# Down-projection of a decoder block on one Trainium2 core: all 22 contraction tiles in seven products, every output tile summed, gated and stored once

## The chip, the cores and the metric

The kernel runs on one core of one Trainium2 chip, in one launch. The metric is the time of an execution on the device in microseconds (us). Three runs of the kernel before gave 660.95, 661.21 and 664.27 us; the median is 661.21.

The core's engines each work through a queue of their own in order: TensorE (PE; its weight loads are shown apart as PEld), VectorE (DVE), ScalarE (ACT), GpSimd (POOL) and SyncE (SP). Here SP issues the plain transfers (hardware queue q1), POOL the accumulating ones, which add what they bring to what lies at the destination (software queue q0). Matmuls write to PSUM, eight banks of 128 x 512 floats; all else lies in SBUF.

## The reference

One layer of a decoder block over 512 tokens of width 1024: modulated norm, an input projection for two kinds of attention heads, an output projection, a gated residual; then a gated MLP with a causal convolution of width 3. The change touches only the last matmul of it, the down-projection of the MLP:

```python
h2 = rmsnorm(x, norm2_w) * (1 + scale2) + shift2
up = causal_dwconv(h2 @ ffn_w_up, ffn_conv_w, ffn_conv_b)
a, b = jnp.split(up, 2, axis=-1)
x = x + gate2 * ((jax.nn.silu(a) * b) @ ffn_w_down)
```

`silu(a) * b` is 512 x 2816, `ffn_w_down` is 2816 x 1024. The contraction of 2816 is 22 tiles of 128.

## The kernel before

**Arithmetic.** All of it is float32. A matmul takes operands of a shorter format (`F32R`), so each operand is split into a high part and a rest, `split(src, hi, lo)`, and a product is made of three passes: high x high, high x rest, rest x high. The high part is a copy (on ScalarE or VectorE, chosen beforehand for each one), the rest a subtraction on VectorE. `split_acc` makes the rest in another way: the negated source is written to the place of the rest, and an accumulating transfer on POOL adds the source in the other form; this takes work off VectorE and puts one transfer of 256 KB on POOL's queue.

**Seven products.** The down-projection pairs contraction tile `k` with tile `k + PAIRS` and splits the tokens (0 to 255, 256 to 511) and the output columns (0 to 511, 512 to 1023) into halves. With `A` the activations and `B` the weights, each as a 2 x 2 block matrix, it forms the four output blocks with seven block products in place of eight (the Winograd form of Strassen's scheme). The code numbers them in the order P1, P2, P5, P6, P3, P7, P4. Each has, for a pair, an `A` operand of 128 x 256 and a `B` operand of 128 x 512, both split, and two chunks of 128 tokens (`c`), each of three matmuls with 512 columns. Each sum over the pairs stays in PSUM. P1, P6, P7 and P4 all go into the two banks `psA`, P5 and P3 into `psB`, P2 into `psC`. When a sum is needed by itself, `snap` copies it out (`y11` after P1, `y22` after P5, `y12` after P6) or subtracts it from an earlier copy (`y22` after P7).

Before, `PAIRS` is 10, so the seven products cover 20 of the 22 tiles. The last two tiles, f = 20 and 21, are done plainly (`down_in`, `down_mm`): each weight tile of 128 x 1024 is loaded whole into the pool `R`, split, and multiplied for eight output tiles (4 token tiles `t` x 2 column halves `j`), on top of the sums that stand in `psC`, `psB` and `psA`, and in a further pair of banks `psD`.

**Output.** `fold` adds the gated copies `y11`, `y12` and `y22` to the residual `x1`; at the end each of the eight output tiles is read from PSUM, multiplied by `gate2`, added to `x1` and stored. The last one, (3, 0), is done in two halves of 256 columns.

**Operands.** `b11`, `b21`, `tw` and `b22` are lists of 128 x 512 tiles, one per pair: the four blocks of `B` and, in `tw` and `b22`, the sums of blocks that the scheme needs, made in place by VectorE or by an accumulating transfer of the weights from DRAM. `sk` and `A21` hold the sums of blocks of `A`. Even pairs of P1, P2, P5 and P6 use `split_acc`. Tiles share 90 SBUF buffers of class `S`, 4 of class `R` and the 8 PSUM banks (class `P`).

**Order.** What sets the order of the work is not the program's loops. The class `_Plan` records every instruction, and `emit` issues them in an order that was planned elsewhere and lies in the file as packed text: `ORDER` (a permutation of all instructions) and `CHOICE` (for each, the first or the second engine). As each engine works in order, this list is the order of every queue:

```python
went = np.cumsum(unpack(ORDER, "<i2").astype(int)).tolist()
second = np.unpackbits(unpack(CHOICE, "u1")).tolist()
return [(self.ops[i], self.ops[i]["how"][second[i]]) for i in went]
```

A buffer is given out in that order too: an instruction that first writes a tile takes the buffer that has been free for longest, and waits for the last reader of what lay in it. The list of before has 6,944 places. Products overlap in it: matmuls of P3 stand between those of P6 and P7, and the plain matmuls of f = 20 and 21 are spread over the last 50 us.

All instructions come from one line of the kernel's text, L281, where `emit` calls the engine; views of the profile therefore tell instructions apart by engine, operation and shape, not by line.

Of the kernel before, what the change touches and what calls it, by code (L numbers as in the profile page):

```python
# [21 lines left out]
P = 128  # L22
# [3 lines left out]
NT = 4  # L26
# [36 lines left out]
c-oD72bdJa^LEwD-t7gBbYzYoASW3_kerktQKDi%5F{xeAQBAtBcli+DCs~Xi6Ek64iH6@=pi{MNK}w~z=hqJuK(LTd&{9d&-  # L63
Xq1?Ci{RcXf4jg}1tUV<_Ms<9uWfblwd{Qw#c9+LJ|JNoQhw)<{q~(M{PZ&*AAyi7;>f|2`GNcctj4FcrYv-
{$uVd5xw^Pr8k#s8F5H<vsMXO8#F|J5z2tB;`=Qv*A*IcSsSsC#6xk5$#9Q7+l|_?YLf&ob)K|6CcG<Je`v`DoQ=+P0`$)m3y)eckSsLjQIxc?t;b{DN
lcjBZcUyY!k1H>AaMomuaD7N)9~b#5YwIqD2qGQ+{fU>voxxjr);wO8iuu{FH%TCFkW4Pzgv;yzxUGHkHTkHI$u_7?kIwD-ua%z{3Uf<p&>$bW4={4xT
lY+~B7eBoq)mel1f!MPt<I;K)bEL8k+*x6#6nF^-
j5n9Ca&ha(q7_xKn^Pzt0`fNXH*qL;n$I6Z`Wn+`}7TrbFX(vAv~$T@k4($Npo30w<PH`$DtD@^Oash+P4X-
J!;5!x)|XVgU*C^PAfq=BpQC{4hqm|`eX{sgy7x#$;ZO_gXT?hit`Q5b0g>cwFOm<r+gCNyq8B%(+Agv_P-XtNPKT$Q@?qcp*|7-MBaF+cq-
H6bP2aL$;k@{qz^$wvVr{S5GVRtkddHPk(Ucd>Z8gkFR0W}?+qyr}~TmdAL{;hNw7XNKnG5@c}E==a}-  # L70
P6D`KawJ0z$ej@7qL`5zkat1Mj@Fb)czaQFU8XeAqp41RKt@Htiwhpg_}6FH^f1Nw4`f6`j#}UU0KM`?L!Jm}%3Cx-evW)Aa}nmUAZhzJhkC~%%VZY8l
Mj8C0Z%sc?@eh;--(6(i;&G171Qp>_L&(HO<n07sYAO!*{1Z!s+lR0BZ7jb%#0`_t9V)y*)Ed}Z95`17(v&_C-
I<~gf|vFLMP=ijg(KNDXhLdT0IxpAy7po(^Fxct^@t*#Y0d(IU*yY9qV@|)r+{^!FZW=MefKPB?o<jf=sO=I|VArl87<^rh%x@gocZ@u^PBv?Mn!Lir=
# [60 lines left out]
07@W;!Z*HIA;YBkNC9lv(VY9CpN7qd3OO<z__dBFvnDQO}ko0L$8IbK!V2(o2yh29%UIS9zrZfs-SZZnTYJuYhm^TZEX-
# [154 lines left out]
def hybrid_block(ctx: ExitStack, tc: tile.TileContext, x, par, ide, cst, adat0, adat, ada1, adag, wg0, wt, wn, ws,  # L289
# [1016 lines left out]
    def snap(pss, sub=None):  # L1306

        plan.sect, out_ = "dnf", sub or [u("sn") for _ in range(2)]
        for c in range(2):
            if sub:  # L1310
                V.tensor_sub(sub[c], sub[c], pss[c])
            else:
                copy(out_[c], pss[c])
        return out_

    def fold(op, ys, i, j):

        plan.sect = "dnf"
        for c in range(2):
# [193 lines left out]
```

## Time and profile before

| what | us |
|---|---|
| three runs | 660.95, 661.21, 664.27 |
| the profiled execution | 661.06 |
| its span, first to last instruction | 659.0 |
| TensorE matmuls busy | 651.9 |
| VectorE busy | 626.8 |
| ScalarE busy | 468.5 |
| POOL busy | 126.5 |

The profiled execution took 661.06 us, of which 659.0 is the span from the first to the last instruction; the 2.06 us around it are not seen in the trace. In the profile, a row of a view by stretches gives for each engine the busy time and, in brackets, the number of instructions that lie in the stretch. `P<-S,S` is an instruction that writes PSUM and reads two SBUF tiles; the name of a class stands for all its tiles. A note such as `[3.26 <-DMA S<-in_wd_dram]` says that the engine was idle for 3.26 us before that instruction, and what ended the wait. Matmuls are pipelined: their mean duration is longer than the distance from one to the next, so the pace is read from how many of them lie in a stretch.

### The profile page before, as it was taken

To read this page: it belongs to the slowest core of one execution; us is meant where nothing else is said; L and a number is where in the kernel's file an instruction comes from. 1 tells how busy PE (TensorE), PEld (TensorE's weight loads), DVE (VectorE), ACT (ScalarE), POOL (GpSimd) and SP (SyncE) were. 2 spreads that over 40 slices of the span, in tenths; PEclk is the share of its full clock that TensorE was granted. 3 is DMA by queue.
4 is the path that set the end of the run, shared out by engine and by line. 5 is a ranking of instruction groups with operands and counts; after the bars stand their busy time and mean duration, and the time that the engine had idled before them with its cause. 6 is when DMAs were issued, how large, how long until landed. Compare 5 with 4: busy or idle time off the path is not lost. (4 is left out here: it accounts for less than half of the span.)

```text
span 659.0 us, 12614 instructions
## 1 busy us (share of the span) xinstructions
PE 651.9 (99%) x4177; PEld 586.6 (89%) x4177; DVE 626.8 (95%) x1540; ACT 468.5 (71%) x1162; POOL 126.5 (19%) x148
## 2 busy tenths in 40 slices
PE   9999999999999999999999999999999999999996
PEld 9887888888988888988999999999999998888775
DVE  7999999988999999999999999999999999999897
ACT  6668896537679999646996466657768789987440
POOL 0001000011000014301113333333332432343200
PEclk9999999999999999999999999999999999999999
DMA  9998646575523579976648899989999999998603
GB/s 320 390 370 288 219 145 185 130 198 129 144 85 108 188 254 233 250 204 203 176 112 164 181 198 187 202 211 211 211 199 199 203 237 257 242 203 178 113 0 129
DMA packets 65609, 129.39 MB, mean 196 GB/s; under 512 B 11124, under 2 KB 11780, under 8 KB 65544
## 3 DMA queue, kind: packets, MB, share of 16 engines
q1 hardware_dynamic: 44920, 91.07, 41.3%
q0 software_dynamic: 20624, 37.52, 34.3%
q8 instruction: 33, 0.54, 0.3%
q14 instruction: 32, 0.26, 0.1%
HBM read 108.11 MB, written 3.41 MB: 169 GB/s over the span
## 5 line engine op out<-in xcount | busy, mean ns | idle before, releaser
L281 PE MATMUL P<-S,S 128*128 128x256 f32 (+5 forms) x3687 | 608.9, 324 | 0.7 <-DVE S L281 0.4
L281 PEld LDWEIGHTS P<-S,S 128*128 128x128 f32 (+3 forms) x3687 | 524.5, 190 | 54.8 <-DVE S L281 1.7
L281 DVE TENSOR_TENSOR S<-S,S 128x512 fp32r<-128x512 f32 (+12 forms) x477 | 240.4, 545 | 5.7 <-ACT S L281 2.2
L281 ACT ACTIVATE S<-S 128x512 fp32r<-128x512 f32 (+3 forms) x345 | 173.6, 548 | 53.2 <-DVE S L281 28.8
L281 ACT ACTIVATE S<-P 128x256 f32<-128x256 f32 (+4 forms) x197 | 79.2, 420 | 55.1 <-PE P L281 52.4
L281 ACT ACTIVATE S<-R 128x512 fp32r<-128x512 f32 (+2 forms) x161 | 90.4, 587 | 20.4 <-PE P L281 10.2
L281 POOL DMA_DIRECT2D S<-R x45 | 42.7, 1003 | 280.3 <-DVE S L281 131.6
L281 POOL DMA_DIRECT2D S<-in_wu_dram x63 | 57.1, 969 | 150.2 <-DVE S L281 79.6
L281 DVE SCALAR_TENSOR_TENSOR S<-S,C,S 128x511 f32<-128x511 f32 (+2 forms) x112 | 81.8, 744 | 0.8 <-ACT S L281 0.2
L281 DVE TENSOR_TENSOR S<-P,S 128x256 f32<-128x256 f32 (+3 forms) x126 | 67.3, 540 | 7.2 <-PE P L281 4.3
L281 DVE TENSOR_TENSOR S<-R,S 128x512 fp32r<-128x512 f32 (+2 forms) x107 | 62.3, 594 | 1.0 <-ACT S L281 0.5
L281 PE MATMUL P<-C,S 128*128 128x128 f32 (+3 forms) x285 | 50.8, 269 | 0.2 <-DMA S<-in_adat_dram 0.2
L281 ACT ACTIVATE S<-S,C 128x512 f32<-128x512 f32 (+1 forms) x70 | 44.0, 646 | 9.1 <-DVE S L281 7.8
L281 PEld LDWEIGHTS P<-C,S 128*128 128x128 f32 (+1 forms) x285 | 36.6, 145 | 7.7 <-issue 0.6
L281 DVE SCALAR_TENSOR_TENSOR S<-S,S 128x512 f32<-128x512 f32 x62 | 41.5, 685 | 0.6 <-PE P L281 0.5
L281 ACT ACTIVATE S<-P,C 128x128 f32<-128x128 f32 (+1 forms) x72 | 29.2, 443 | 15.2 <-PE P L281 11.9
L281 ACT ACTIVATE S<-S,s 128x128 f32<-128x128 f32 (+4 forms) x82 | 38.1, 496 | 2.1 <-DVE s L281 1.6
L281 DVE SCALAR_TENSOR_TENSOR S<-P,C,S 128x511 f32<-128x511 f32 (+3 forms) x52 | 32.9, 650 | 0.9 <-PE P L281 0.5
L281 POOL DMA_DIRECT2D S<-S x20 | 17.5, 935 | 46.7 <-ACT S L281 42.7
L281 ACT ACTIVATE S<-P,C,C 128x128 f32<-128x128 f32 (+2 forms) x38 | 18.2, 519 | 8.4 <-DVE C L281 3.2
L281 DVE TENSOR_TENSOR S<-S,P 128x256 f32<-128x256 f32 (+1 forms) x36 | 16.8, 467 | 2.3 <-PE P L281 1.7
L281 PE MATMUL P<-R,S 128*128 128x512 f32 (+2 forms) x72 | 18.7, 364 | 0.0
(79 smaller groups left out, 300.9 us busy)
## 6 DMA issues: line engine op xcount, KB each, us to landing
S<-in_adat_dram SPq DMA_DIRECT2D x64, 256.0 KB
S<-in_wu_dram POOLq DMA_DIRECT2D x63, 256.0 KB, 5.4
R<-in_wu_dram SPq DMA_DIRECT2D x23, 512.0 KB
S<-R POOLq DMA_DIRECT2D x45, 256.0 KB, 5.6
S<-in_wu_dram SPq DMA_DIRECT2D x42, 256.0 KB
S<-in_wd_dram SPq DMA_DIRECT2D x40, 256.0 KB
S<-in_adag_dram SPq DMA_DIRECT2D x32, 256.0 KB
R<-in_wn_dram SPq DMA_DIRECT2D x12, 512.0 KB
```

The costliest lines, as they stand in the source:

```text
L281: getattr(engines[eng], method)(*map(place, args), **{k: place(v) for k, v in kw.items()})
```

## The change

`PAIRS` goes from 10 to 11, so all 22 tiles go through the seven products. The plain part (`down_in`, `down_mm`, `psD`, the raw loads of f = 20 and 21) is removed. Each output block is finished by a new helper `finish` where its sum is complete in the program's text: `y11 + psC` for block (0, 0), `psB - y12` for (0, 1), `y22` for (1, 1), and `psA` for (1, 0). It multiplies by `gate2`, adds to `x1` and stores; `fold` is removed. In the last product, P4, the operands of the last four pairs (`TAIL`) are made first, then their matmuls run chunk by chunk, the second chunk in two halves of 256 columns, each finished and stored by itself.

`ORDER` and `CHOICE` are replaced. The new list has 6,966 places; its first 5,125 are those of the old one. Its last weight load (`b22[7]`) stands at place 6,572; in the old list the last one (`b22[9]`) stands at 6,700. The diff, without the packed texts and cut where nothing is changed in substance:

```diff
-    PAIRS, LATE = 10, 2
+    PAIRS, TAIL = 11, 4
...
-    def prod(pss, k, a, b_, first, acc=False):
+    def prod_in(a, b_, acc):
         plan.sect = "dnw"
-        w = plan.tile("S", (P, 512), F32R, "w"), u("wl", F32R) if acc else plan.tile("S", (P, 512), F32R, "w")
+        w = u("w", F32R), u("w", F32R)
         (split_acc if acc else split)(b_, *w)
         plan.sect = "down"
         x_ = u("da", F32R)
-        ah, al_ = x_[:, :256], x_[:, 256:]
-        split(a, ah, al_)
+        split(a, x_[:, :256], x_[:, 256:])
+        return x_, w
+
+    def prod_mm(ps, k, c, x_, w, first, n=slice(0, 512)):
+        ah, al_ = x_[:, c * P:c * P + P], x_[:, 256 + c * P:256 + c * P + P]
+        for i, (l_, r_) in enumerate(((ah, w[0]), (ah, w[1]), (al_, w[0]))):
+            T.matmul(ps[:, n], l_, r_[:, n], start=first and k == 0 and i == 0, stop=k == PAIRS - 1 and i == 2,
+                     skip_group_check=True)
+
+    def prod(pss, k, a, b_, first, acc=False):
+        ins = prod_in(a, b_, acc)
         for c in range(2):
-            for n, (l_, r_) in enumerate(((ah, w[0]), (ah, w[1]), (al_, w[0]))):
-                T.matmul(pss[c], l_[:, toks[c]], r_, start=first and k == 0 and n == 0, stop=k == PAIRS - 1 and n == 2,
-                         skip_group_check=True)
+            prod_mm(pss[c], k, c, *ins, first)
...
-    def fold(op, ys, i, j):
-
+    def finish(y, i, j, c, n=slice(0, 512)):
         plan.sect = "dnf"
-        for c in range(2):
-            x_ = x1[2 * i + c][j]
-            V.tensor_mul(ys[c], ys[c], gate2[j])
-            getattr(V, op)(x_, x_, ys[c])
+        t, x_ = 2 * i + c, x1[2 * i + c][j]
+        o = u("uy") if y.tensor.name.startswith("P") else y
+        V.tensor_mul(o[:, n], y[:, n], gate2[j][:, n])
+        V.tensor_add(x_[:, n], x_[:, n], o[:, n])
+        Q.dma_start(out[t * P:(t + 1) * P, j * 512 + n.start:j * 512 + n.stop], x_[:, n])
...
         prod(psC, k, A12[k], b21[k], True, k % 2 == 0)
+    for c in range(2):
+        plan.sect = "dnf"
+        V.tensor_add(y11[c], y11[c], psC[c])
+        finish(y11[c], 0, 0, c)
...
+    for c in range(2):
+        plan.sect = "dnf"
+        V.tensor_sub(y12[c], psB[c], y12[c])
+        finish(y12[c], 0, 1, c)
...
     snap(psA, y22)
-    for k in range(PAIRS):
+    for c in range(2):
+        finish(y22[c], 1, 1, c)
+    for k in range(PAIRS - TAIL):
         prod(psA, k, A22[k], tw[k], False)
-    for op, ys, i, j in (("tensor_add", y11, 0, 0), ("tensor_sub", y12, 0, 1), ("tensor_add", y22, 1, 1)):
-        fold(op, ys, i, j)
-    psD = [bank("psd") for _ in range(2)]
...
-    def down_in(f):
-        raw, w = load_raw(wd[f]), []
...
-    def down_mm(f, t, j, w, ah, al_, c=slice(0, 512)):
...
-            V.tensor_mul(tmp[:, c], psd[t, j][:, c], gate2[j][:, c])
-            V.tensor_add(tmp[:, c], tmp[:, c], x1[t][j][:, c])
-            Q.dma_start(out[t * P:(t + 1) * P, j * 512 + c.start:j * 512 + c.stop], tmp[:, c])
+    ins = [prod_in(A22[k], tw[k], False) for k in range(PAIRS - TAIL, PAIRS)]
+    for c in range(2):
+        for n in (slice(0, 256), slice(256, 512)) if c else (slice(0, 512),):
+            for k in range(TAIL):
+                prod_mm(psA[c], k + PAIRS - TAIL, c, *ins[k], False, n)
+            finish(psA[c], 1, 0, c, n)
```

More of the change, by code (lines that the diff above doesn't have):

```diff
@@ L69 @@
[L69 to L73, printed above, removed]
@@ new lines @@
+~drXLBT`7BPls&IKqXU>H5FjGk2W+e4g)n_SxB)=~P`^;jQZ4XiAM3?R*yK>%1R|q9(LfUL-
+|pq#ZFn>m?*@>9%Z_SMc<egxR<Mf1h&ccf}|{m~!Fnn*CiNy=kg+p}TmB^y_>nA7GrX<^R=dJIY3fq%`Wcvs9YzF3Cp^q&P}9qx~ovjqCfg6W5E9g`T2
+)5~R!&OJ^lB<)<z*SPXS%<bmwN-
+HY@M=6nlx_tD2GDMOdUkvw!=c8FKTbWTdpo3uz$Bom&p;F~Cm(4w=YDJRv#b*D_sK>d4kLL#UTMNl$+wVabD&`YZ1$D0W7BS2;Fdjn-
+BBpT(}>8gZN3D9sJV?}_DQglbO{0*8-FWEp(L2xKl%=`^cBPa^9P69<iI*NW;<9Zh@A~44>QXOk~3-fT~f|wDjP#DF78@VU|>RgQSn><ZLaUY-qQUTZV
+^1ZaAyd-i~ic%8BVLFCuUg{`Yv2uB7BPccNl`M5=tJFoCMf{S!Abn*z-
@@ new lines @@
+m}}#iR8roEi0)W~TQ%m=krhy(@zi>8!uRH3imvi5?h;vr?ax-=n4QbTO2y^HE)Ti}FZ-
+E5O%8(Oq4djE0_&tf)C#>hLGf`_1XSm$lbutEW3{9i}D0ZlJwB=c3OnPZf2CHR_N1bHP%&xs#v2=ZDVJuzjJmkiG)J_>kd4`GA)5&SV)7NOYpnZ+GcSN
+t7A(p&jqgwfP~u+)q5#c^5WbgQAeC>r6=>-
+FS<P_cgeap2d@7DBa{jdJF$S5o%DVz0nhD8djA$xUp`EM1m6;+aFcAD8hZz+eO(B)*>~U&Z=?huaGz61$>kyxJ&p^s|xxM7t_bkx1(a+TdIY=0sGht&)
+<R9tAT?QY;ml<&0A#{bk|^!{;H1Ck_~S}`lv5l1+P$)e$}6cRmb>!(e^a@Opu#=-
+^m;Z*Ei6rtUk}N`iwrI?oey@p033nML+2}EK*C}_EE)mdU>F+<I$FbYv5T+3tr9{`SXnanQQCGcsIbVrJ+Nm%i#-
+ZljXv<kct;*qi)XgtPHuZ{P_c!+^2XB=W>IA{dUFkqi#E1qm$sl&Z}t1N-
@@ new lines @@
+`^qyMJ>)D<bv0+}2m*d7iFIKr?Q0e(S?-
+x~JtuNLzE<7ots)D0Lv!vk<R5bocWaSgBp~TDmnm#U2vh6t*(7)Y=Av?aI?`)ab^wc{3e$4ohaNXAxa2uv9lTx&V}ONX&fymITBL&1?_%-
+3Q?12`*^u>mH-2sw!P|OR5c0RM%DqvCf5gm99dmZnR3W6rAA#I=gyI-
+{Hp~DVw<@#fOznttlqz$VV59{OTVh8&{H#xf`(#@kuJ}dg!klpVE1OPl}5m;@cy&184PlH@neVpjVP>IyY~{44=|Z(`;*L-
+ogA5EUh7lFmac<;9iwKSxXF?nB#FBkT~nfuzu(xi0}8P*G=z`2J{O(EgMvB-
+I@!)8%AiCZ^9DiP(k`Y8aXFbd0kDeswt4)5ju|Isg6@82>ce>9SA~yVx1~#JO{~qO48H%3w|-
+UA=Fa`XcE6mi>0fciqde%eo6Y+VvTXm;DGtf7EBCn(}l6Z&vPx?ey1(3hr6!$#z|9p(Mpq|@95Xi_`rJlTqXnUd<Bm8<7pV<J|7RYQ)}EDnAt~xEAp9B
@@ new lines @@
+5xum|;%g=3%L7ePP&#-pgQ1U>gh{?D;3y-
+tN(sx6u%dZw^v)!B9XK8rd&P2;w^q#QY*UU^etnW*d_aXPYq)vLz_aX))O^HkfZxety@<8(PSn2Bxq`X5L6vWWf;-FQ5;%BjL3W#Z1`U<qN`w-pD9-
+X_0C(9c6##rhrOX)V=zl?81eyHC-
+r1?0oaI9_fIrWK{o_takOD{6}F<yTU+{3C}dcXNOJ2ZWT)un>z)Gm}a4TjWr=rMVk*^l>Y_@%}QnBQvh6R+15xF#fhy39vZdXh?@WM{;p<jxUmQ)W50)
+K<O0u95lN)l(rWLzBa4OayqHY-aqM%@8(?cqaMhh!)9{v6k)a&hHJ|rmN)Tv0`*OLCXC@4iDIj;5#-
+G{1Q3Pp|{24b_d84uuI3(c^L|<aWH+JH{9$2vkUd7wRRI_j~+=?fh-
+%+D*49NdXi_#Jiq<|$Z$Qs<qrF<zP(=rwAVul@p)}5Xd&oSeScrU`)tq)(MxUl46Pt?|InYWrMo{Xlck84cc2~9*^9(mleaVY8h(vGYK=AY_G8&*1kC+
@@ new lines @@
+k@KO&Y#_AyZHb36(Jtt-ur?<U!gzq=!5nBD{&e{rzGkGALYIY)djGlrB+{Qg(tjX34y*)=e-
+Mch}N7;8%A#2&`pst9>v^Z>gLB614fL>qZ)nce0Z?h>kWB@!*J)3o7pIY{*GWhKZ{M>J1EFs&>`6S9Dec3hHJhOKU-
+P|XJ596o^o{Pu`UJS|1OZj1^cFIc@WqX>HBz0sp{DQZeS{RW@v+$$Ik!-
+BXT>4Ev%`0V#j^syP*x1>}=mpwA#qGN{aQzY<ZWZqTpi0sXdS&cOCojiG2J?=m1ihT1=!}?%Vq6A31|WTo&CPd}X^^Gb62(;|v$X@8L}RS1(DYSi|BbW
+A0GUFUv<^&mChA$BaRIfK-
+C@mBb5Soc=M?^X7j&mYp?xpwIi|aPl$XuRPmBEW6y4OG2w`dhzfcNMN+~WON&aa9v+w)~@UPjEFi&YdE)lkLDPp0gfeMYEHj=&EU8R`zat&S6YFh%Ln-
+&&9?Ex|}=RU#%A;-f|7t!m#Dg8*kq@&`!e?0xI+24-lw5Qc#^r`3n%(55#4B1YiS@3+`DlMhcavJwVA*W_{-
@@ new lines @@
+rFzgY;DtMT>C)EytcP=EPM8|5o~ZfnFWb9v%M!-
+sE#iwEz%Kyk<iD}EfTOLP4Vx$&>uS9T8AdGl^RM9T5mk79#4ybN2i<q5p^7pZdRsCS=%28AAUs}3|7qgg#EC*W_HVD6l|@rx7C2u*Yh@=rm@+ry?%@?1
+L<`_<X8@PWG@|&y8fvQgIBx2`Yez~^PNMp@wAc*KU$@);VgC3Eg{=!2o;i=*1Ma?y_R2^$x6i}scfIRa-5vkk9vH@ueHmrWfdUOC%C(ODV+>It@n7-
+?ngHiv##?Y-<7zLy$_-68#$*7bJ~u=vnE@c&d)3U-
+Ew?iNq;+u&dO5IQcu63=5g_KpZ~J1&h4RLW;gsCO}GAVmU#JQv)AL*s;rK<$$nplsDgh&Yc4E)1xh=qut+*1zNw!<rsBkK+MJk~C4K)>w|<c(YO7nup1
+t|^ry~4on)i5<%uZIU(@B|K$bvd;rg`nzn0|;Ddh$%Y4fcE<^eU_D=1n@EdXL049(%nkgr}@)DNV~t7-
@@ new lines @@
+IVadIP@5%lpLuJ!O|LPO!)+C(zn;eVb<T*E%aLWf!_UlY8s8q2DoNV&tc}5S0VoG-u+sA%gz}vDIxkrANW9-
+<S8TSGeP^U?!lf*}%Zd^f+E(CH16SLVTADjAwT29K1Uvcclg_cP(gfCaMHvHw#j>8d3b`b{@dW;Nve+9Z^&S{fe0c;3M|os;t*sD;sea1wNdl+q$EFO5
+dES4WlISb`KW8XS!$|pdOgt6?+P}s>P?u`sL-aoHj{AXwwq-
+FmM0HvFAVyf9C@22I!`KnI}V%X2=6E`QH9C2U-+kb@L<fX8R=9mz`MUs)&U;VWs;5F%Fg-pe_vknSB>mwt?^Ftokt6(2wL(dZ35H9u>yCE?W*6ibnu3G
+@#t{K(x$}TZpw!YjeKX1z)%0cQfS1WLw9I7gG$vJPa=R4EmZRk)Sz<-
+fvrJkFaOzy*&Ddz)v1`CQ3nACgUZ4r^Ucjm*puj92;u?KVzb%uJ*qzZNMjGv)_4b&M6Z;+LP%EIeL~lqFqbqr`dPeg%PJo9h-
@@ L184 @@
 c-muNfPnxOMg~%V11^aMBGtix08~`~36>B59156Xj0_?`n;IOT90-Py5J!73u;6tlir1K+E>vKGc>)F?mM>@k8O!0(F*%J<!T=`6%7o-
[L185 to L186 removed]
+QY~JHQ7hu9A!2pji7IXoqj~Wo73JeJh2VgP+U?;*uf&*r{0;+ie*j&d5brc6wPXp8fCPa)mpa%t7s!+fYzARXMiQ!`woGH=)H4GduLkeoW1Gbb(C?Y7x
+9sp><5Z(
 """
@@ L1366, in hybrid_block @@
     snap(psA, y22)
-    for k in range(PAIRS):
+    for c in range(2):
+        finish(y22[c], 1, 1, c)
+    for k in range(PAIRS - TAIL):
         prod(psA, k, A22[k], tw[k], False)
-    for op, ys, i, j in (("tensor_add", y11, 0, 0), ("tensor_sub", y12, 0, 1), ("tensor_add", y22, 1, 1)):
-        fold(op, ys, i, j)
-    psD = [bank("psd") for _ in range(2)]
-    psd = {(2 * i + c, j): ((psC, psB), (psA, psD))[i][j][c] for i in range(2) for j in range(2) for c in range(2)}
-    plan.sect = "down"
@@ L1375, in down_in @@
-    def down_in(f):
-        raw, w = load_raw(wd[f]), []
-        for j in range(2):
-            w.append((plan.tile("S", (P, 512), F32R, "w"), plan.tile("S", (P, 512), F32R, "w")))
-            split(raw[:, j * 512:j * 512 + 512], *w[j])
-        ah, al_ = u("ah", F32R), u("al", F32R)
-        split(act[f], ah, al_)
-        return w, ah, al_
-    def down_mm(f, t, j, w, ah, al_, c=slice(0, 512)):
-        (lh, ll), (rh, rl), o = (ah[:, toks[t]], al_[:, toks[t]]), (v[:, c] for v in w[j]), psd[t, j][:, c]
-        T.matmul(o, lh, rh, start=f == 2 * PAIRS and t > 1 and j == 1 and c.start == 0, stop=False, skip_group_check=True)
-        T.matmul(o, lh, rl, start=False, stop=False, skip_group_check=True)
-        T.matmul(o, ll, rh, start=False, stop=f == NF - 1, skip_group_check=True)
@@ L1390, in hybrid_block @@
-    for f in range(2 * PAIRS, NF - LATE):
-        ins = down_in(f)
-        for t in range(NT):
-            for j in range(2):
-                down_mm(f, t, j, *ins)
-    ins = [down_in(f) for f in range(NF - LATE, NF)]
-    for t, j in ((0, 0), (1, 0), (0, 1), (1, 1), (2, 1), (3, 1), (2, 0), (3, 0)):
-        last = (t, j) == (3, 0)
-        tmp = u("uy")
-        for a in (0, 256) if last else (0,):
-            c = slice(a, a + 256) if last else slice(0, 512)
-            for f in range(NF - LATE, NF):
-                down_mm(f, t, j, *ins[f - NF + LATE], c)
-            V.tensor_mul(tmp[:, c], psd[t, j][:, c], gate2[j][:, c])
-            V.tensor_add(tmp[:, c], tmp[:, c], x1[t][j][:, c])
-            Q.dma_start(out[t * P:(t + 1) * P, j * 512 + c.start:j * 512 + c.stop], tmp[:, c])
+    ins = [prod_in(A22[k], tw[k], False) for k in range(PAIRS - TAIL, PAIRS)]
```

197 lines of the change are left out of this document (81 added, 116 removed).

## The prediction

> **What bounds the kernel now.** I read the page's first part, then the table by stretches, then the timeline around the one place where TensorE pauses, the chain that ended last, and the timeline of the end.
>
> ```profile
> span 659.0 us, 12614 instructions
> PE 651.9 (99%) x4177; PEld 586.6 (89%) x4177; DVE 626.8 (95%) x1540; ACT 468.5 (71%) x1162; POOL 126.5 (19%) x148
> ```
>
> TensorE is busy for 99% of the span and VectorE for 95%. Both shares hide stages, so the next view cuts the part that the change touches. Its columns are the stretch, its length, then busy time and number of instructions of PE, PEld, DVE, ACT and POOL, the granted clock, the DMA engines' share and GB/s.
>
> ```profile
> 473.60:654.00 180.40, 179.95 (x1080) 160.30 (x1078) 176.77 (x357) 127.32 (x264) 51.58 (x59) 1.00 0.80 179
> 500.00:540.00 40.00, 40.00 (x336) 40.00 (x334) 39.45 (x79) 31.77 (x63) 14.85 (x17) 1.00 0.97 212
> 540.00:621.00 81.00, 81.00 (x383) 68.06 (x382) 79.47 (x172) 67.39 (x146) 28.01 (x32) 1.00 0.95 213
> 560.00:620.00 60.00, 60.00 (x266) 49.69 (x266) 59.54 (x129) 47.74 (x102) 22.62 (x26) 1.00 0.94 201
> 620.00:625.00 5.00, 4.61 (x20) 3.17 (x19) 3.43 (x8) 2.29 (x5) 0.00 (x0) 1.00 0.13 24
> 625.00:630.00 5.00, 5.00 (x24) 4.13 (x23) 5.00 (x10) 2.38 (x5) 0.00 (x0) 1.00 0.00 0
> 621.00:641.00 20.00, 19.61 (x83) 15.08 (x82) 19.43 (x39) 9.22 (x21) 0.00 (x0) 1.00 0.01 1
> ```
>
> The packed issue orders of the two kernels agree in their first 5,125 places, and behind them the old list has 1,078 matmuls. The row from 473.60 to 654.00 has that many (and two that overlap its edges), so the first 473.6 us stay as they are and all gains or losses fall behind that point.
>
> The row 560 to 620 is the down-projection at full pace: 266 matmuls of 512 columns in 60.00 us, 0.2256 us each. The row 500 to 540 is the up-projection: 336 of 256 columns in 40.00 us, 0.119 us each. A matmul costs by its columns, with 0.012 us more where 512 columns are cut in two (2 x 0.119 - 0.2256). The clock is 1.00 in every row. TensorE sets the pace; at that pace 20 us hold 88.7 matmuls, and the row 621 to 641 has 83. So 5.7 x 0.2256 = 1.28 us are lost to waits there. Most of it is one event: 620 to 625 has 20 matmuls, 625 to 630 has 24, and 4 x 0.2256 = 0.90 us. The timeline says why,
>
> ```profile
> 620.87 1.77 ACT L281 ACTIVATE S<-S 128x512 fp32r<-128x512 f32 x4 [3.26 <-DMA S<-in_wd_dram]
> 621.53 2.90 DVE L281 TENSOR_TENSOR S<-S,S 128x512 fp32r<-128x512 f32 x6 [1.93 <-ACT S L281]
> 623.22 30.73 PE L281 MATMUL P<-S,S 128*128 128x512 f32 x138 [0.39 <-DVE S L281]
> ```
>
> and the chain, in order of time:
>
> ```profile
> 612.64 8.15 DMA S<-in_wd_dram
> ...
> 620.87 0.64 ACT S L281
> 621.51 0.02 issue
> 621.53 1.64 DVE S L281 x3
> 623.17 0.04 issue
> 623.22 30.03 PE P L281 x132
> ```
>
> The last weight tile (`b22[9]`) is asked for at 612.64, when a buffer comes free, and lands 8.15 us later. ScalarE stood 3.26 us for it, VectorE 1.93 us, TensorE only the 0.90 us that its lead did not cover. After that the chain is TensorE to the end of the products.
>
> **Part 1, the matmuls.** Before: 10 pairs x 7 products x 2 chunks x 3 passes = 420, and 2 single tiles x 8 output tiles x 3 = 48, so 468 of 512 columns, six of them cut in two. After: 11 x 7 x 2 x 3 = 462, twelve of them cut in two. The number of instructions stays 474. Saved: 6 x 0.2256 = 1.35 us; six more cuts cost 6 x 0.012 = 0.07. Sum: **-1.28 us**, on the path, as TensorE has nothing else to wait for.
>
> **Part 2, the operand work on VectorE and ScalarE.** Counted from the two texts and the packed choices, the down-projection's VectorE work goes from 112 instructions of 512 columns and 120 of 256 to 102 and 128; ScalarE's from 99 and 64 to 105 and 74.
>
> ```profile
> L281 DVE TENSOR_TENSOR S<-S,S 128x512 fp32r<-128x512 f32 x53 | 35.3, 685 | 1.9 <-ACT S L281 1.9
> L281 DVE TENSOR_TENSOR S<-S,S 128x256 fp32r<-128x256 f32 x62 | 24.2, 417 | 0.1
> L281 ACT ACTIVATE S<-S 128x512 fp32r<-128x512 f32 x80 | 46.5, 621 | 13.9 <-DVE S L281 9.4 <-DMA S<-in_wd_dram 3.4 <-PE P L281 0.8
> L281 ACT ACTIVATE S<-S 128x256 fp32r<-128x256 f32 x56 | 20.9, 405 | 1.3 <-PE P L281 0.8 <-DVE S L281 0.4
> ```
>
> VectorE: -10 x 0.685 + 8 x 0.417 = -3.5 us. ScalarE: 6 x 0.621 + 10 x 0.405 = +7.8 us, into an engine that was idle for 13.6 of the 81 us from 540 to 621. Neither is on the path while its lead lasts, so I count both at nothing; without that cover the bounds are -3.5 and +7.8 us. VectorE, the nearer to its limit (79.47 of 81), gets lighter. The new early sums out of PSUM make no wait for it: in the new list `y11 + psC` stands 112 places behind the last matmul of product 2, and `psB - y12` 42 behind the last of product 3 in its chunk, and no operand of a matmul hangs on them. I take zero.
>
> **Part 3, the transfers.** Loads by SP bring the same bytes: 40 of 256 KB and two of 512 KB before, 44 of 256 KB after. The eleventh pair has an even number, so it adds four accumulating transfers on POOL for the low halves of products 1, 2, 5 and 6, and two that add a weight tile: 6 more than the 32 that POOL issues from 540 to 621.
>
> ```profile
> q0 software_dynamic: 4838, 8.80, 62.9%
> q1 hardware_dynamic: 4470, 8.40, 32.2%
> ...
> S<-S POOLq DMA_DIRECT2D x17, 256.0 KB, 5.8
> S<-in_wd_dram POOLq DMA_DIRECT2D x15, 256.0 KB, 7.9
> ```
>
> In that stretch POOL's queue took 62.9% of 81 us for 8.80 MB, that is 50.9 us for 33.6 transfers of 256 KB, 1.52 us each. Six more are **9.1 us of all sixteen engines**, in a stretch whose DMA share is already 0.95. From 621 to 641 the share is 0.01, so there is room behind. What of it reaches TensorE lies between nothing and 9.1 us. Nearest row: 81 us at share 0.95 cost TensorE 0.90 us, so I take nothing and keep the rest as a rival. By the Trainium skill ("DMA: Bandwidth & Descriptors", Specifications) the fabric moves 435 GB/s, which would make such a transfer 0.60 us and the six 3.6 us, an estimate; the trace's 1.52 us is two and a half times that, and I go by the trace.
>
> **Part 4, the wait at 621.** In the new order the last weight load stands 394 places from the end of the list; in the old one it stood 244 from it, in the middle of POOL's last transfers. No load is left that late, and the two whole 512 KB tiles with it are gone. I take the 0.90 us of that event as won, and leave the other 0.38 us of the 1.28: **-0.9 us**. Bounds: all 1.28 goes, or as much is lost elsewhere.
>
> **Part 5, the end.** From the timeline of the last microseconds:
>
> ```profile
> 650.76 3.19 PE L281 MATMUL P<-S,S 128*128 128x256 f32 x18
> ...
> 653.27 0.69 DVE L281 TENSOR_TENSOR S<-P,S 128x512 f32<-128x512 f32 x1 [0.19 <-PE P L281]
> 654.00 0.69 DVE L281 TENSOR_TENSOR S<-S,S 128x512 f32<-128x512 f32 x1
> 654.61 0.42 DVE L281 TENSOR_TENSOR S<-P,S 128x256 f32<-128x256 f32 x1
> 655.06 0.42 DVE L281 TENSOR_TENSOR S<-S,S 128x256 f32<-128x256 f32 x1
> ...
> 650.98 4.86 SPq L281 DMA_DIRECT2D out_dram<-S  x5
> ```
>
> TensorE ends at 650.76 + 3.19 = 653.95, VectorE at 655.48: 1.53 us, because only six half matmuls (0.7 us) stand behind the tile before the last one, whose gating takes 1.34 us (653.27 to 654.61). In the new code twelve half matmuls stand there (four pairs x three passes): 12 x 0.119 = 1.43 us cover the 1.34, and only 0.42 + 0.42 + 0.02 = 0.86 us follow TensorE. **-0.67 us**. The new order ends so: matmuls, then multiply, add and store of the last 256 columns. Behind it stay 659.0 - 655.48 = 3.5 us for the last 128 KB store. Five stores go out from 650.98 on, three of 256 KB and two of 128 KB; the last five of the new list are the same, so I leave it. All nine stores stand behind place 6,900 of the new list, which costs nothing: SP has no load behind them.
>
> **Sum.** -1.28 - 0.90 - 0.67 = -2.85. Span 659.0 - 2.85 = 656.15; the profiled execution took 661.06, 2.06 over its span, so **658.2 us**. The median of the three runs, 661.21, is 0.15 above that execution. A measurement of this kernel tells 0.5% (3.3 us) from no change, so faster means under 657.9 and slower over 664.5: my forecast lies just inside "no change".
>
> **Rivals.** (a) *All waits go.* VectorE is lighter by 3.5 us and the loads are earlier, so all 1.28 us vanish: 661.06 - 1.28 - 1.28 - 0.67 = 657.8, and down to 656.8 if the last store meets a quieter queue (1 of its 3.5 us, which is my allowance). For it: one cause made 0.90 of 1.28. Against: new orders bring small waits of their own. Chance 0.27.
>
> (b) *A new wait at the hand-over of a PSUM bank.* Products 6, 7 and 4 all go into the banks `psA`, and the result of product 7 must be read by VectorE before product 4 may go on. Before, 48 single-tile matmuls with banks of their own (48 x 0.2256 = 10.8 us of work) could be put into that gap; now only the shift between the two chunks covers it. Price, if nothing covers: a read of 0.675 us and one instruction of 0.68 us ahead of it, some 1.4 us for each chunk:
>
> ```profile
> 634.32 0.68 DVE L281 TENSOR_TENSOR S<-P,S 128x512 f32<-128x512 f32 x1
> 634.92 0.67 DVE L281 TENSOR_TENSOR S<-S,P 128x512 f32<-128x512 f32 x1
> ```
>
> That gives 658.2 + 1.4 to 2.8 = 659.6 to 661.0. Against it: six product matmuls of the other chunk hide 1.35 us each time. Chance 0.20. The Trainium skill ("Perfetto Trace Analysis", Matmul Optimizations) asks that all eight PSUM banks be used; the old code uses eight here, the new one six, so by that rule it would go this way. No run here shows it yet.
>
> (c) *Slower: the transfers become the pace.* Place: products 1, 2, 5 and 6, from 540 to 600, where the share is 0.95 and a transfer of 1.52 us takes 5.8 to 7.9 us to land, so a queue stands ahead of each. The four added transfers there delay all loads behind them by 4 x 1.52 = 6.1 us; it decides once that is more than the lead of the loads. Then 661.06 + 6.1 - 1.28 - 0.67 = 665.2. Against it: TensorE runs without a gap through the whole stretch, and ScalarE stood for a weight load 3.4 us in all. Chance 0.10.
>
> (d) *It doesn't save matmul time*, because the number of instructions stays at 474: if each cost the same whatever its columns, part 1 would be nothing and the time 659.5. The 0.119 us of the 256-column rows speak against it. Chance 0.03.
>
> **Numbers.** Forecast 658.2, chance 0.40 for 657.9 to 659.2. The range leaves out (c) and the far edges: 656.8 to 662.5. Faster by over 0.5%: (a) and a little of the forecast, 0.30. Slower: (c), 0.10. Within: the rest, 0.60.
>
> **What would show it.** Matmuls of the last stage 450 of 512 columns and 24 of 256; after 473.6 us no 5 us stretch with 20 matmuls where 24 fit; ScalarE's wait for `in_wd_dram` near 621 gone; VectorE ending 0.9 us behind TensorE. Wrong if TensorE shows gaps in 540 to 600 behind ScalarE or a transfer (c), or one behind a VectorE read of PSUM some 20 us before the end (b).

## The result and the profile after

The changed kernel takes 658.53 us (median of 20 executions), the kernel before 662.45 us on the same chip (20 executions): ratio 0.9943, 95% interval 0.9924 to 0.9962. That is 0.57% faster, or between 0.38 and 0.76%, where the forecast of 658.2 us stood for 0.46%. The bound of 0.5% lies inside the interval, so the runs don't say on which side of it the change falls. Nine of the 20 executions before and six of the 20 after are some 2.5 to 5 us longer than the rest, the six with a mean granted clock of 0.991 to 0.994 where the rest have 0.998 or more (no clock is on record for the 20 before); the medians of the rest are 661.31 and 658.29 us, which makes the change 3.0 us or 0.46%. The profiled execution of the changed kernel took 657.67 us, 1.77 of it around its span.

The page of the changed kernel begins so (busy time, share of the span and instructions of each engine), and its rows of the two busy DMA queues (packets, MB, share of sixteen engines) follow:

```profile
span 655.9 us, 12653 instructions
PE 648.8 (99%) x4177; PEld 584.7 (89%) x4177; DVE 623.1 (95%) x1537; ACT 474.0 (72%) x1179; POOL 132.0 (20%) x154
...
q1 hardware_dynamic: 45208, 91.07, 41.1%
q0 software_dynamic: 21488, 39.09, 36.3%
```

TensorE and VectorE are both down, by 3.1 and 3.7 us, with the same number of matmuls. ScalarE is up by 5.5 us and POOL has its six more transfers. The table by stretches (same columns as for the kernel before):

```profile
500.00:540.00 40.00, 40.00 (x333) 39.81 (x332) 38.47 (x77) 31.34 (x65) 15.18 (x18) 1.00 0.99 210
540.00:621.00 81.00, 81.00 (x384) 68.08 (x383) 80.91 (x179) 72.23 (x159) 28.82 (x33) 1.00 0.96 214
560.00:620.00 60.00, 60.00 (x266) 49.70 (x265) 59.92 (x136) 52.38 (x116) 23.63 (x27) 1.00 0.94 192
620.00:625.00 5.00, 5.00 (x23) 4.13 (x22) 5.00 (x13) 4.80 (x13) 3.21 (x4) 1.00 0.54 89
625.00:630.00 5.00, 5.00 (x23) 4.13 (x22) 5.00 (x10) 3.39 (x8) 0.33 (x1) 1.00 0.96 157
621.00:641.00 20.00, 20.00 (x90) 16.57 (x89) 20.00 (x40) 9.64 (x22) 3.54 (x4) 1.00 0.33 55
```

The row 620 to 625 had 20 matmuls and has 23; the row 621 to 641 had 83 and has 90, as many as fit. TensorE's busy time is the whole stretch in each row. In the column of VectorE one reads what became important later: 80.91 of 81 us. Before, it was 79.47, but 1.40 of the 1.53 us that were missing are VectorE's own wait for the late load (the 1.93 us that ended at 621.53). So VectorE was as good as full in this stretch in both kernels.

The timeline has one unbroken block of matmuls from 599.63 on, and the list of waits from 540 us (idle for, us in total, times, longest) has only 0.3 us in which ScalarE stands for a weight load, where 3.4 us stood before:

```profile
599.63 51.82 PE L289 MATMUL P<-S,S 128*128 128x512 f32 x239
```

```profile
ACT S L289 <- DMA S<-in_wd_dram: 0.3, 1, 0.3
```

The end, by the timeline:

```profile
647.77 3.67 PE L289 MATMUL P<-S,S 128*128 128x256 f32 x22
647.88 4.85 SPq L289 DMA_DIRECT2D out_dram<-S  x7
...
650.05 0.69 DVE L289 TENSOR_TENSOR S<-P,S 128x512 f32<-128x512 f32 x1 [0.33 <-PE P L289]
650.78 0.69 DVE L289 TENSOR_TENSOR S<-S,S 128x512 f32<-128x512 f32 x1
651.48 0.42 DVE L289 TENSOR_TENSOR S<-P,S 128x256 f32<-128x256 f32 x1
651.94 0.43 DVE L289 TENSOR_TENSOR S<-S,S 128x256 f32<-128x256 f32 x1
```

TensorE ends at 647.77 + 3.67 = 651.44. The gating of the tile before the last one (650.05 to 651.47) is done as TensorE ends, and VectorE ends at 652.37, 0.93 us behind. The chain that ended last says the same: TensorE alone from 249 us, then four instructions of VectorE.

```profile
249.24 400.80 PE P L289 x2764
650.05 0.70 DVE S L289
650.78 0.69 DVE S L289
651.48 0.44 DVE S L289
651.94 0.43 DVE S L289
```

**Where the time went.** Traces are compared from place 5,100 of the issue order, just ahead of where the two lists part, because the part before it, alike in all of them, took 471 to 476 us (the last section says why). In the table, "TensorE" is the time from the start of that instruction to the end of the last matmul, "lost" the sum of its pauses: the time by which a matmul started later than the steady pace of one behind another (0.2268 us with 512 columns, 0.1199 with 256), where that is over 0.03 us, and "tail" how long VectorE ends behind TensorE. They are worked out from the trace's records of single instructions.

| kernel | median, us | ratio to before on the same chip, 95% interval | TensorE, us | lost, us | tail, us |
|---|---|---|---|---|---|
| before | 662.45; 661.40; 661.66; 661.53 | | 182.46 | 1.25 | 1.54 |
| changed | 658.53 | 0.9943, 0.9924 to 0.9962 | 180.10 | 0.29 | 0.92 |
| e1_matmuls12 | 661.18 | 0.9992, 0.9963 to 1.0021 | 182.53 | 0.00 | 0.92 |
| e2_early_load | 659.73 | 0.9957, 0.9930 to 0.9984 | 181.07 | 0.00 | 1.54 |
| e3_acc6 | 660.52 | 0.9978, 0.9952 to 1.0004 | 184.93 | 4.98 | 0.93 |
| e4_dve6 | 661.74 | 1.0000, 0.9974 to 1.0027 | 183.86 | 3.78 | 0.92 |
| e5_tail6 | 659.22 | 0.9957, 0.9925 to 0.9989 | 181.56 | 1.63 | 1.53 |
| e6_handover | 659.79 | 0.9964, 0.9941 to 0.9986 | 182.08 | 2.20 | 0.93 |
| e7_dve6_late | 662.84 | 1.0006, 0.9977 to 1.0035 | 182.94 | 2.92 | 1.31 |
| e8_early_dve6 | 662.79 | 1.0021, 0.9994 to 1.0047 | 184.25 | 2.98 | 1.54 |
| e9_act6 | 658.92 | 0.9960, 0.9934 to 0.9986 | 181.36 | 1.40 | 0.93 |
| e10_dve3 | 659.39 | 0.9962, 0.9940 to 0.9984 | 181.60 | 1.32 | 0.92 |

The four medians of the kernel before belong to the changed kernel's runs, to e1 to e4, to e5 to e8, and to e9 and e10. They differ by up to 1 us, so a difference below between the medians of an experiment and of the changed kernel is good to 1 us at best, and the columns on the right carry the sizes. They come from one execution of each kernel.

From before to changed the span went down by 3.1 us: TensorE by 2.36, the tail by 0.62, and 0.13 lie ahead of place 5,100, where the lists are alike. The last store took 3.5 us in both. Of TensorE's 2.36, the cheaper set of matmuls is 1.28 (twelve of 512 columns fewer, twelve of 256 more: 12 x (0.2268 - 0.1199)) and the pauses are 0.96: the 1.25 us from 621 to 636 are gone, and three pauses of 0.1 us at 508 to 510 stand in this execution. The 0.12 that is left are delays under 0.03 us each. That is the whole difference; what the experiments had to tell was which edit stands behind each of these parts, and why the costs that the prediction counted at nothing stayed out.

### The profile page after: what moved, and what is told of

It reads as the page before. It is cut to its first block, busy times and chain, and to the rows that moved or that the text cites. A ratio compares the mean times of both kernels' runs of the same rounds, so it can differ in the third digit from the quotient of the medians.

```text
span 655.9 us, 12653 instructions
## 1 busy us (share of the span) xinstructions
PE 648.8 (99%) x4177; PEld 584.7 (89%) x4177; DVE 623.1 (95%) x1537; ACT 474.0 (72%) x1179; POOL 132.0 (20%) x154
## 4 chain that ended last, share of the span: by engine, by line
PE 93%; ACT 3%; DVE 2%; DMA 1%; SPq 1%; issue 0%
PE P L289 93%; ACT S L289 2%; DVE S L289 2%; DMA S<-in_adat_dram 1%; SPq L289 1%; ACT L289 0%; DVE s L289 0%; ACT s L289 0%; DVE C L289 0%
## 5 line engine op out<-in xcount | busy, mean ns | idle before, releaser
L289 DVE TENSOR_TENSOR S<-S,S 128x256 fp32r<-128x256 f32 (+12 forms) x484 | 241.0, 542 | 4.9 <-ACT S L289 1.5
L289 ACT ACTIVATE S<-S 128x512 fp32r<-128x512 f32 (+3 forms) x363 | 180.7, 546 | 57.1 <-DVE S L289 36.1
L289 ACT ACTIVATE S<-R 128x512 fp32r<-128x512 f32 (+2 forms) x156 | 87.6, 586 | 18.8 <-PE P L289 7.4
L289 DVE TENSOR_TENSOR S<-P,S 128x256 f32<-128x256 f32 (+3 forms) x122 | 64.8, 537 | 7.8 <-PE P L289 5.0
L289 DVE TENSOR_TENSOR S<-R,S 128x512 fp32r<-128x512 f32 (+2 forms) x103 | 59.6, 591 | 1.0 <-ACT S L289 0.5
L289 POOL DMA_DIRECT2D S<-S x24 | 21.5, 936 | 46.0 <-ACT S L289 28.1
L289 POOL DMA_DIRECT2D S<-in_wd_dram x17 | 17.4, 1207 | 18.2 <-DVE S L289 10.9
L289 DVE TENSOR_TENSOR S<-S,P 128x256 f32<-128x256 f32 (+1 forms) x38 | 18.2, 478 | 2.7 <-PE P L289 2.4
```

The lines of the kernel that those rows point to most:

```text
L289: getattr(engines[eng], method)(*map(place, args), **{k: place(v) for k, v in kw.items()})
```

## The experiments

All experiments run beside the kernel before; e2 and e8 are made from it, the others from the changed kernel. Where instructions are added, their results aren't read.

**e1_matmuls12: are TensorE's columns on the path?** Twelve matmuls of 512 columns behind place 6,600, into a bank that nothing else uses.

```diff
+    spare = bank("spare")
+    for _ in range(12):
+        T.matmul(spare, held[0][:, :P], held[1][0], start=True, stop=True)
     plan.emit(pools)
```

> The changed kernel with twelve matmuls of 512 columns more, into a PSUM bank that nobody reads, behind product 3's fourth pair (about 40 us before the end); nothing else is added. If the end is set by TensorE's columns (the theory behind the -1.28 us of the forecast): +12 x 0.2256 = +2.7 us on the span of 655.9, so 658.6, and no gap on TensorE. If other engines or transfers set the end and TensorE has slack beside them: less than +1 us.

TensorE takes 182.53 us in place of 180.10, 2.43 more, with nothing lost and the tail unchanged. The twelve follow one another at 0.226 to 0.227 us, 2.72 in all; the 0.29 that the changed kernel's profile lost at 508 to 510 us does not occur here, which is the difference. Its timeline has one block to the end:

```profile
559.78 94.20 PE L256 MATMUL P<-S,S 128*128 128x512 f32 x426
```

What is added to TensorE reaches the end in full. The saving of six matmuls' worth of columns is real, and that the number of instructions stays the same (rival (d)) doesn't matter.

**e2_early_load: was the late load alone the cause of the wait?** The kernel before, with its last weight load put into a buffer of class `R` and moved from place 6,700 to 6,489.

```diff
-        dst[k] = u("wd")
+        dst[k] = plan.tile("R", (P, 512)) if (k, j, f) == (9, 1, 19) else u("wd")
```

> The kernel before, with one edit: the last weight tile b22[9] gets a buffer of the class R, which has room there, and its load stands in the list behind that of b22[5], so it is asked for near 594 us and not at 612.6. VectorE, POOL and the matmuls stay as they are. If the wait at 621 came from that late load: no stretch near 621 with 20 matmuls where 24 fit, span 659.0 - 0.9 to 1.2 = 657.8 to 658.1. Rival, the wait was VectorE's fullness or POOL's bunched transfers from 608 to 613, and went because VectorE became lighter: the gap stays, span 658.7 to 659.2.

Nothing is lost on TensorE any more: 181.07 us, 1.39 less than before, and by the medians 1.7 us less. The rows of its table by stretches, 600 to 620 and 620 to 640, and the timeline:

```profile
600.00:620.00 20.00, 20.00 (x90) 16.58 (x89) 20.00 (x43) 14.04 (x31) 6.19 (x7) 1.00 0.84 144
620.00:640.00 20.00, 20.00 (x90) 16.54 (x89) 19.57 (x40) 7.06 (x16) 0.00 (x0) 1.00 0.00 0
```

```profile
599.65 52.38 PE L255 MATMUL P<-S,S 128*128 128x512 f32 x236
```

There are 90 matmuls from 620 to 640 where the kernel before has 84. VectorE has as much work as before and the tail is 1.54, so the wait goes by the load alone, with nothing taken off VectorE. The small losses at 632 and 635 us, which the prediction left standing, went with it: they were the same late load, seen further on.

**e3_acc6: how near are the transfers to being the pace?** The changed kernel with six more accumulating transfers of 256 KB on POOL (and three memsets of their destinations), at the places of products 1, 2 and 5: the change's own six doubled.

```diff
+    more = [plan.tile("R", (P, 1024)) for _ in range(3)]
+    for m in more:
+        G.memset(m, 0.0)
+    for i in range(6):
+        G.dma_start(more[i // 2][:, i % 2 * 512:i % 2 * 512 + 512], wd[i][:, :512], accum_op=OP.add)
     plan.emit(pools)
```

> The changed kernel with six accumulating transfers of 256 KB more on POOL's queue between products 1 and 6 (weights from DRAM, into spare buffers of class R that nobody reads), and three memsets on POOL ahead of them: as much transfer work again as the change added, 6 x 1.52 = 9.1 us of all engines. If the loads have a lead there (the forecast): span 655.9 to 656.9. If the transfers are near the pace (rival c): up to 4 x 1.52 = 6.1 us more, 658 to 662, with TensorE waiting between 560 and 610.

Median 660.52, 2.0 us above the changed kernel (2.3 by the two ratios). In the timeline VectorE stands 2.43 us for a transfer from `in_wd_dram`, and TensorE 1.80 us for VectorE:

```profile
570.47 1.70 DVE L256 TENSOR_TENSOR S<-S,S 128x512 f32<-128x512 f32 x4 [2.43 <-DMA S<-in_wd_dram]
...
574.10 4.45 PE L256 MATMUL P<-S,S 128*128 128x512 f32 x11 [1.80 <-DVE S L256]
```

```profile
574.00:578.00 4.00, 3.90 (x10) 2.75 (x11) 3.37 (x9) 3.42 (x7) 1.76 (x2) 0.57 1.12 247
578.00:582.00 4.00, 4.00 (x19) 3.29 (x18) 3.84 (x10) 3.19 (x9) 1.76 (x2) 1.00 1.09 223
```

In the rows by stretches behind that wait there are 10 matmuls in 4 us, then 19, and the granted clock is 0.57, then 1.00. So this profiled execution lost 4.98 us, more than the median. The way of rival (c) exists, and it opens with six transfers more than the change has; its price here is 2 us and not 6.1, since two loads in that stretch were late (issued at 562.81 and 564.39, waited for until 570.47 by VectorE and 574.58 by ScalarE) and not all. The run doesn't tell the DMA engines' share from POOL's own time: the six transfers and three memsets also took 11.1 us of POOL.

**e4_dve6 and e10_dve3: has VectorE room?** The changed kernel with six (e4) or three (e10) additions of 512 columns on VectorE, spread over the stretch from about 553 to 584 us.

```diff
+    for _ in range(6):
+        V.tensor_add(plan.tile("R", (P, 512)), x1[3][0], x1[3][1])
     plan.emit(pools)
```

> The changed kernel with six VectorE additions of 512 columns more (3.6 to 4.1 us, results that nobody reads), spread over places 6,100 to 6,350 of the list, that is over some 25 us of products 1 and 5: it gives VectorE back the 3.5 us that the change took from it. If VectorE has a lead over TensorE (the forecast counts the 3.5 us at nothing): span 655.9 to 656.4, and no gap. If its lightening is what removed the waits: TensorE waits again for VectorE, +1 to +4 us, 657 to 660.

> The changed kernel with three more additions of 512 columns on VectorE (3 x 0.69 = 2.1 us) at every other place of e4_dve6; their results are not read. If VectorE has no lead beyond some 0.5 us, about 1.6 us are lost (0.69 x 3 less the lead), 660.1 us, with pauses of TensorE that VectorE ends. If it has a lead of some 2 us that six additions used up, nothing is lost: 658.5.

e4 takes 661.74, 3.2 us more than the changed kernel, and TensorE 3.76 us more; e10 takes 659.39, 0.9 more, and TensorE 1.50 more. The additions are 4.2 and 2.1 us of work on VectorE. The rows from 560 to 600 of the changed kernel, then of e4, then the row from 560 to 580 of e10:

```profile
560.00:580.00 20.00, 20.00 (x90) 16.57 (x89) 20.00 (x44) 17.65 (x40) 7.74 (x9) 1.00 1.00 234
580.00:600.00 20.00, 20.00 (x90) 16.57 (x89) 20.00 (x49) 16.67 (x37) 8.90 (x11) 1.00 0.99 192
```

```profile
560.00:580.00 20.00, 19.15 (x82) 14.90 (x81) 20.00 (x41) 16.75 (x35) 7.43 (x9) 1.00 1.01 243
580.00:600.00 20.00, 19.51 (x85) 15.48 (x85) 20.00 (x49) 15.54 (x34) 8.44 (x10) 1.00 0.86 167
```

```profile
560.00:580.00 20.00, 19.81 (x86) 15.52 (x85) 20.00 (x42) 16.15 (x36) 6.45 (x8) 1.00 0.94 216
```

VectorE is busy for all of 20 us in each row, and TensorE goes from 90 matmuls to 86 and 82. The lists of waits name the engine (first e4, then e10; the changed kernel has no such row):

```profile
PEld P L256 <- DVE S L256: 4.8, 9, 0.9
```

```profile
PEld P L256 <- DVE S L256: 2.3, 6, 0.6
```

The expectation that a lead covers this falls. Worked out from single records, the shortest time between the end of an operand's split and the matmul that reads it was 0.4 to 0.7 us in each 10 us of the changed kernel from 550 to 620. That is VectorE's whole lead at the tightest operands, and 2.1 us of work more than use it up.

**e9_act6: is that so of any engine, or of VectorE?** The same places, but six copies of 512 columns on ScalarE (3.7 us).

```diff
+    for _ in range(6):
+        S.activation(plan.tile("R", (P, 512)), x1[3][0], AF.Copy)
     plan.emit(pools)
```

> The changed kernel with six more copies of 512 columns on ScalarE (6 x 0.62 = 3.7 us), spread over the same places as the six extra VectorE additions of e4_dve6; their results are not read. If only VectorE is level with TensorE, ScalarE (72% of the span) takes them: 658.5 us as without them, no new pause on TensorE, up to 0.5 us for copies that now come later. If any engine's work ahead of the matmuls counts in this stretch, because the operands are made just in time whoever makes them, the loss is as in e4_dve6: some 3 us, 661.5.

Median 658.92, 0.4 above the changed kernel. Of the 1.40 us lost in its trace 0.65 lie at 473 and 524 us, ahead of the copies; 0.53 at 565 fall among them, and 0.22 at 609 and 614 behind them. The row from 560 to 580, and the row of its list of waits that names ScalarE:

```profile
560.00:580.00 20.00, 19.74 (x88) 16.01 (x87) 20.00 (x42) 19.17 (x42) 6.99 (x8) 1.00 1.01 223
```

```profile
PEld P L256 <- ACT S L256: 0.7, 1, 0.7
```

ScalarE takes 3.7 us more for 0.4 us by the medians and 0.5 to 0.8 by the trace; VectorE took 4.2 us more at the same places for 3.2 and 3.8. The copies write the same buffers as the additions and read one of their two sources, so these are not the cause. ScalarE's share of part 2 was rightly counted at nothing.

**e8_early_dve6: was VectorE level before the change as well?** The kernel e2 (before, with the early load) with six additions on VectorE at the times of e4.

> e2 (the kernel before with the early load) with the same six VectorE additions at the same times as in e4, near 553 to 581 us. If the eleventh pair ate VectorE's lead there (5 us of splits and sums more in products 1, 2 and 5): e2 has more room than the changed kernel, 0 to +1 us. If VectorE stood level with TensorE before the change too: +3 to +4 us on e2, as in e4.

Median 662.79, 3.1 us above e2, and TensorE 3.18 us more. Its rows show the same picture as e4's:

```profile
560.00:580.00 20.00, 18.60 (x81) 14.69 (x80) 19.97 (x42) 16.99 (x36) 6.05 (x7) 1.00 1.03 257
580.00:600.00 20.00, 19.62 (x85) 15.54 (x84) 19.97 (x43) 16.05 (x33) 6.62 (x8) 1.00 0.82 170
```

So VectorE had no room in the old order either. Whether a change that took columns off TensorE and left VectorE's work as it was would have met that limit was not run.

**e7_dve6_late: is it so towards the end too?** The changed kernel with the same six additions at places 6,785 to 6,869, from 627 to 640 us.

> The changed kernel with the six VectorE additions of e4 placed late, between 627 and 640 us, where the change took the gating and folding away, so VectorE has the total of before again. e4 cost 3.2 us by the medians. If VectorE is a second limit that stands level with TensorE up to the end: +2.0 to +3.5 us here too. If e4 only hit a thin place in products 1, 2 and 5 and the end has room: 0 to +0.6 us.

The median is 662.84, but the executions spread from 659.88 to 666.28, so the trace is the better measure: from place 5,100 TensorE takes 2.84 us more and the tail 0.39, together 3.2. The timeline has TensorE standing for VectorE:

```profile
636.40 5.44 PE L256 MATMUL P<-S,S 128*128 128x512 f32 x20 [0.17 <-DVE S L256]
642.82 5.53 PE L256 MATMUL P<-S,S 128*128 128x512 f32 x23 [0.98 <-DVE S L256]
```

VectorE has no room here either: in neither of the two stretches tried, 553 to 584 and 627 to 640 us, is added work on it caught up.

**e5_tail6: does the number of half matmuls behind the second last tile set the tail?** Six of the last twelve half matmuls (places 6,946 to 6,951 of the unpacked list) are moved ahead of that tile's last ones, so that six stay behind it, as in the kernel before.

```diff
-order[6941:6952]
+order[6946:6952] + order[6941:6946]
```

> The changed kernel with six of the last twelve half matmuls moved ahead of the last matmuls of the chunk before, so that only six stand behind that chunk, as before the change; no instruction more or less. If the forecast's part 5 is right: TensorE ends where it did, VectorE ends 1.5 us behind it and not 0.93, span +0.6 to 0.7. If VectorE would have been done in time anyway: no change.

```profile
647.78 4.97 PE L256 MATMUL P<-S,S 128*128 128x512 f32 x29
...
652.07 0.69 DVE L256 TENSOR_TENSOR S<-P,S 128x512 f32<-128x512 f32 x1 [0.89 <-PE P L256]
...
653.86 0.43 DVE L256 TENSOR_TENSOR S<-S,S 128x256 f32<-128x256 f32 x1
```

In the timeline of the end TensorE stops at 652.75 and VectorE at 654.29: 1.54 us, the tail of the kernel before. The median is 0.7 us above the changed kernel, as a tail longer by 0.61 would have it, though this cannot be told from the medians alone: the profiled execution also lost 1.63 us, 0.84 of it at 473 us and all of it ahead of the edit.

**e6_handover: what does the hand-over of a PSUM bank cost if nothing covers it?** In the first chunk of tokens, product 4 follows product 7 in one bank. Six matmuls that need neither (four of product 4 in the other chunk, two of product 3) stand between the two; they (`moved`: places 6,843, 6,844, 6,847, 6,848, 6,853 and 6,854) are put behind the first three of product 4.

```diff
-order[6843:6858]
+[o for o in order[6843:6858] if o not in moved] + moved
```

> The changed kernel with the six matmuls that stand between product 7's end and product 4's start in the first chunk moved behind product 4's first three; no instruction more or less. It uncovers the hand-over of the bank psA (rival b). If the cover is what hides it: one gap on TensorE of 0.9 to 1.5 us near 636 (drain, what VectorE has at hand, the subtraction of 0.68), span +0.9 to +1.5. If the hand-over costs nothing by itself: no gap.

The timeline of TensorE, then of VectorE, around the place:

```profile
631.63 5.15 PE L256 MATMUL P<-S,S 128*128 128x512 f32 x22
637.70 4.59 PE L256 MATMUL P<-S,S 128*128 128x512 f32 x19 [0.92 <-ACT S L256]
```

```profile
636.87 0.68 DVE L256 TENSOR_TENSOR S<-S,P 128x512 f32<-128x512 f32 x1
```

TensorE stands from 636.78 to 637.70 while VectorE reads the sum of product 7 out of PSUM, until 637.55. The note names ScalarE, but it is VectorE's read that had just ended. Counted from start to start of the matmuls it is 1.16 us of the 2.20 lost; the rest lies at 541 and 553 to 555 us, ahead of the edit. The median is 1.3 us above the changed kernel. The price of rival (b) is real, and in the change as made those six matmuls cover it.

## Why the prediction was right, and where its reasons were not

**Part 1 (-1.28): right.** Twelve matmuls of 512 columns at 0.2268 us became twelve of 256 at 0.1199, 1.28 us, and e1 shows that such columns reach the end. The reason given, that TensorE has nothing else to wait for, held only narrowly, as part 2 shows.

**Part 2 (counted at nothing): the zero came out, its reason did not.** "Neither is on the path while its lead lasts" was not checked, and for VectorE that lead is some half a microsecond: 2.1 us more of work cost 1.5 us of TensorE, 4.2 us more cost 3.8 (e10, e4), in the old order too (e8). VectorE is a second limit, level with TensorE. The row with VectorE busy for 79.47 of 81 us had been quoted and read as "nearer to its limit"; nearly all that was missing there was VectorE's own wait for the late load, so it stood at its limit. By the page it has 3.7 us less to do now (-3.5 counted). That wasn't needed for part 4, since in e2 the wait went with VectorE's work as before. For part 1 no run shows what would have come of it with VectorE's work unchanged; with 4.2 us put back, the whole gain is gone (ratios 1.0000 in e4 and 1.0006 in e7), though that doesn't restore the old state: the same work costs the old order as much (e8). That no term was missing here was therefore partly luck. For ScalarE the step was right (e9). Of its +7.8 us the page shows 5.5: the packed choices also take three copies of 512 columns of the up-projection off it and put four of 256 on it, about -0.4 net, and copies that follow one another overlap in the records (129 of 0.621 us, 80.1 in sum, are 75.6 us of busy time), so that counts times mean durations come out too high.

**Part 3 (nothing of 9.1 us): right for this change, by a small margin.** All transfers are in time here, and six more of the same kind cost 2 us (e3).

**Part 4 (-0.90): right in its cause, off in size.** The late load cost TensorE 1.39 us (e2), and the 0.38 us that were left out of 1.28 had the same cause, so rival (a)'s count was nearer here. Even 1.28 was low: a row counts the matmuls across its edges too, so the 83 should have been set against the 90 that a full row of 20 us shows and not against 88.7 (such a count is good to one matmul either way), and the pace is 0.2268 us and not 0.2256. Small waits elsewhere, the argument against (a), did show: 0.29 us at 508 to 510 in the profile of the changed kernel (its row from 500 to 540 has 333 matmuls where the kernel before has 336), though e1, with the same order, has none there.

**Part 5 (-0.67): right.** -0.62, for the reason given (e5). The last store, left alone, took 3.5 us as before.

**Rivals.** (b) did not come; its price of 1.4 us for a chunk was measured as 0.9 to 1.2 (e6). The rule of the Trainium skill ("Perfetto Trace Analysis", Matmul Optimizations) that all eight PSUM banks be used would have had the change lose here; with six banks TensorE has no pause behind place 5,560, at 509.8 us, so in this kernel the trace goes against it. (c) did not come; its mechanism showed with double the transfers. (d) is refuted by the paces of 0.2268 and 0.1199 us in one trace. The parts sum to -3.0 of span where -2.85 was forecast (the late load 0.49 too small, the new pauses 0.29 the other way); 0.13 lie in the common part and 0.29 outside the span (2.06 to 1.77). Profiled, that is 657.67 us against 658.2.

## What to carry to other kernels

Where two engines are both busy for nearly all of a stretch, ask of each edit what it does to both: here 4.2 us of work put back on VectorE took the whole saving on TensorE away, and the time from an operand's last step to its use, not the share of busy time, tells whether there is room. A single stall behind a load is mended by giving that load a buffer that is free earlier; one moved load (e2) took 1.4 us off TensorE, where the whole change took 2.4. At the end, let as many matmuls follow the second last tile as its gating takes.

## What the runs showed of the hardware

A pause of TensorE of under 2 us was followed by half pace: in e3, after 1.80 us without a matmul, the clock row of the next 4 us is 0.57 and ten matmuls fit where nineteen fit after; the delays behind the first matmul add up to 1.8 us. Pauses of 0.9 to 1 us (e6, e7) had no such effect: the granted clock stays at 1.00 in their stretches. The Trainium skill ("TensorE: Matmul & The Clock Gate", Part 1: The HAM clock gate) puts the drop behind an idle window of about 3.4 us; the pause here was half as long. So a short wait can cost its own length again.

The clock of the first 100 us differs from one execution to the next: 1.00 in the profile of the changed kernel, 0.95 in that of e8, whose shared first part is 5 us longer (place 5,100 starts at 476.34 against 471.35). The rows are those of the changed kernel and of e8:

```profile
0.00:100.00 100.00, 97.47 (x530) 81.19 (x531) 93.84 (x266) 77.73 (x205) 2.65 (x7) 1.00 0.82 286
```

```profile
0.00:100.00 100.00, 96.99 (x501) 81.92 (x502) 89.04 (x258) 72.92 (x190) 2.64 (x7) 0.95 0.82 285
```
